# Toeplitz tables laid out once in DRAM, one load per readout table, and six of eight state copies on VectorE

## The chip, the core and the metric

The kernel runs on one core of a Trainium2 chip. TensorE (PE in the rows) does the matmuls, VectorE (DVE) and ScalarE (ACT) the elementwise work, GpSimd (POOL) a little of it, and SyncE (SP) issues every DMA of this kernel, in program order on one queue. The metric is the time of the whole kernel on the device in microseconds, lower is better. Three runs of the kernel before took 742.02, 746.75 and 749.24 us, a median of 746.75.

## What is computed

One layer of a backbone over 1024 positions of width 1024, in float32. Each large matmul is done on operands split in a high and a low half, three matmuls for one (hi times hi, hi times lo, lo times hi). Cut to what matters here:

```python
h = layer_norm(x) * (1 + scale) + shift
ua, za, ub, vb, zb, ga, gb = split(h @ w_in + b_in)      # widths 512 x5, 1024 x2
# branch a: a bidirectional state space over positions, 32 groups of 16 channels, 64 complex states
y  = s5_bidir(ua)                                        # y = D*u + C s (forward) + C s (backward)
ya = (g := gelu(y)) * sigmoid(g @ glu_w + glu_b) * silu(za)
# branch b: a gating unit in chunks of 128 positions
v  = layer_norm(gelu(vb)) * ln_g + ln_b
yb = gelu(ub) * (w_s @ v + b_s) * silu(zb)
m  = sigmoid(ga) * (ya @ w_a) + sigmoid(gb) * (yb @ w_b)
out = layer_norm(alpha * x + gate * (m @ w_out + b_out)) * ln_g2 + ln_b2
```

## The kernel before

The state space is computed in blocks of 8 positions: a scan over 160 blocks on VectorE carries the states, and within a block the output is a small Toeplitz matrix times the inputs. The projections are done in blocks of 128 output channels (`proj`: two halves of 512 positions, 24 matmuls each into one PSUM bank, `pp<block><half>`). The blocks are numbered: UB is 0 to 3, ZB 4 to 7, ZA 8 to 11, GA 12 to 19, GB 20 to 27. In the order of the program:

- The adaLN and the projection of `ua`, then UB+0 and UB+1 with the inputs of the states (`v_in`, `v_out`), which fill `vst`, the state buffer.
- UB+2 and UB+3 with the tables of the readout. `out_powers(b)` writes the output powers `kca` of channel block b to a DRAM table `cad` (512 KB for each of two directions). `kernels(b, d)` makes the Toeplitz rows in PSUM (`pk`), copies them into `wk` on ScalarE (L651, L652) and VectorE (L655, L656), and stores them to the DRAM table `wd`.
- `scan(1, 50)`: 49 steps of three VectorE instructions each (L608, L611, L612).
- The `vb` projection with positions as rows: 192 matmuls (L690 to L692) into all eight PSUM banks at once (`pvb0` to `pvb7`), so that the next projection needs a bank that an eviction has freed. Then for each of the eight banks, the evacuation with a bias on VectorE (L698), gelu on ScalarE (L699) and a layer norm (`norm_rows`: statistics on VectorE, a few small ones on GpSimd, the scaling on ScalarE, L189).
- ZB+0 and ZB+1 (`pp40`, `pp41`, `pp50`, `pp51`), with a Silu on ScalarE that goes into `zt` (L568), the gating unit (`prs` and `ps` matmuls, L712 and on), and ZB+2, ZB+3.
- The eight steps of branch b's gate (`branch(i, GB, ...)`, TensorE) over the rest of the scan (VectorE).
- The readout. `y_tables(b)` loads what one channel block needs: `ca` (two loads of 512 KB from `cad`), `mt` (the Toeplitz table; eight loads of 64 KB from `wd`, each of which spreads shifted rows over 16 partitions) and `um` (the inputs; two loads of 256 KB). `y_states(b)` copies the states out of `vst` into `z`, eight copies of 64x512 per b, four on ScalarE and four on VectorE. `y_mm(b)` does 16 times [`um` times `mt`, `z` times `ca` twice] on TensorE (L801, L803), and a gelu into `gk` on ScalarE (L805). `y_trans(b)` transposes `gk` (L813). Then ZA, the half-GLU, GA, the output projection and the last layer norm.

Weights come through `weights(key, ahead)`: a load into a `RAW` buffer, a ScalarE copy that rounds to the high half `h_` (L72), and a VectorE subtraction that gives the low half `l_` (L73). `WSP` has 6 buffers for the halves, `RAW` has 3, `G` 27, `ROW` 2 and `TMP` 4. The program is written in one order; a scheduler places the instructions on each engine's queue, and an engine takes its queue strictly in order. A DMA can start no sooner than its destination buffer is free and its turn on SyncE's queue has come.

Of the kernel before, what the change touches and what calls it, by code (L numbers as in the profile page):

```python
# [8 lines left out]
F32 = mybir.dt.float32  # L9
F32R = mybir.dt.float32r  # L10
I32 = mybir.dt.int32
AF = mybir.ActivationFunctionType
# [4 lines left out]
T = 8  # L17
# [9 lines left out]
UB, ZB, ZA, GA, GB = 0, 4, 8, 12, 20  # L27
# [8 lines left out]
def mixer_kernel(ctx: ExitStack, tc: tile.TileContext, a, out):  # L36
    nc = tc.nc
    V, S, Pl, PE = nc.vector, nc.scalar, nc.gpsimd, nc.tensor
# [3 lines left out]
    dram = ctx.enter_context(tc.tile_pool(name="dram", bufs=1, space=bass.MemoryType.DRAM))  # L42

    def pool_of(tag, bufs, dshape, ddt=F32):
        def make(name, shape=dshape, dt=ddt):
            return sb.tile(list(shape), dt, name=name, tag=tag, bufs=bufs)
        return make

    G = pool_of("g", 27, (128, 1024))
    BIG = pool_of("big", 1, (128, 2 * NSLOT * 32))  # L50
    RAW = pool_of("raw", 3, (128, 1024))
    WSP = pool_of("wsp", 6, (128, 1024), F32R)
    TMP = pool_of("tmp", 4, (128, 512))
    ROW = pool_of("row", 2, (128, 1280))
# [5 lines left out]
    def BANK(name, shape=(128, 512)):  # L60
        return psum.tile(list(shape), F32, name=name, tag="b", bufs=8)

    def dma(o, i):
        nc.sync.dma_start(o, i)
# [22 lines left out]
    def emit_load():  # L87
        key, ap, shape, eng = jobs[emitted[0]]
        emitted[0] += 1
        raw = RAW("r_" + key, shape)  # L90
        dma(raw, ap)
        hi, lo = WSP("h_" + key, shape), WSP("l_" + key, shape)
        split(hi, lo, raw, eng)
        loaded[key] = (hi, lo)

    def weights(key, ahead=2):
        i = [j[0] for j in jobs].index(key)
        while emitted[0] < min(i + 1 + ahead, len(jobs)):
            emit_load()
        return loaded[key]  # L100
# [154 lines left out]
    ud = dram.tile([4, T, 128, 160], F32, name="ud")  # L255
# [71 lines left out]
    q, w, z, sn, cs, odd, eve, sg = (r_[i] for i in range(3, 11))  # L327
# [128 lines left out]
    for j in range(2):  # L456
        t = RAW(f"xc{j}")
# [36 lines left out]
    for b in range(4):  # L494
        p = BANK(f"pcu{b}")
# [69 lines left out]
    def act_into(blk, fn, dst=None, then=None, ahead=None, mid=None):  # L565
        def evac(p, sl):
            t = dst[:, sl] if dst is not None else TMP("act")
            S.activation(t, p, fn, bias=cols[:, C_BLK + blk:C_BLK + blk + 1])  # L568
            if then is not None:
                then(t, sl)  # L570
        proj(blk, evac, ahead, mid)
# [4 lines left out]
    vm = [G("vm0")]  # L576
# [41 lines left out]
    mask = C("mask", [128, 16])  # L618
    V.tensor_reduce(mask, ident.rearrange("p (j h) -> p h j", h=16), axis=AX.X, op=OP.add)
    wd = dram.tile([32, 16, 240], F32, name="wd")  # L620

    cad = dram.tile([4, 2, 128, 1024], F32, name="cad")
    kca = {}

    def out_powers(b):
        for d in range(2):
            ca = G(f"kca{b}{d}", (128, 8, 8, 16))
            outer(ca, ROW("katmp", (128, 8, 8, 16)), V, pc, xcr, xci, b, d, OP.subtract)
            dma(cad[b, d], ca.rearrange("p g i h -> p (g i h)"))
            kca[b, d] = ca  # L630
# [3 lines left out]
    def kernels(b, d):  # L634
        if d == 0:
            pks[b] = BANK(f"pk{b}", (128, 2, 256))
        pk = pks[b]
        ca = kca[b, d]
        gg = 32 * d + 8 * b
        for k in range(4):  # L640
            for par in range(2):
                lh = bbar[:, gg + 2 * k:gg + 2 * k + 2, :].rearrange("p g h -> p (g h)")
                o = pk[32 * k:32 * k + 32, par, :]
                g = 2 * k + par
                PE.matmul(o[:, 128 * d:128 * d + 112], lh, ca[:, g, d:d + 7, :].rearrange("p i h -> p (i h)"),
                          start=True, stop=True)
                PE.matmul(o[:, 128 * d + 112:128 * d + 128], lh, xcr[:, gg + g, :], start=True, stop=True)
        if d == 0:
            return
        wk = TMP(f"wk{b}", (128, 2, 240))  # L650
        S.activation(wk[:, :, 0:112], pk[:, :, 128:240], AF.Copy)  # L651
        S.activation(wk[:, :, 128:240], pk[:, :, 0:112], AF.Copy)  # L652
        dm = TMP(f"dm{b}", (128, 3, 16))
        V.tensor_scalar(dm[:, 2, :], mask, cols[:, C_D + b:C_D + b + 1], None, op0=OP.mult)
        V.tensor_tensor(dm[:, 0:2, :], pk[:, :, 112:128], dm[:, 2, :].unsqueeze(1).to_broadcast([128, 2, 16]), op=OP.add)  # L655
        V.tensor_tensor(wk[:, :, 112:128], pk[:, :, 240:256], dm[:, 0:2, :], op=OP.add)  # L656
        for g in range(8):
            dma(wd[8 * b + g], wk[16 * g:16 * g + 16, g % 2, :])

    for i in range(2, 4):  # L660
        vm.append(G(f"vm{i}"))
    out_powers(0)
    out_powers(1)
    act_into(UB + 2, AF.Gelu_apprx_tanh, dst=vm[2])
    kernels(0, 0)
    kernels(0, 1)
    out_powers(2)
    kernels(1, 0)
    kernels(1, 1)
    out_powers(3)  # L670
    act_into(UB + 3, AF.Gelu_apprx_tanh, dst=vm[3], mid=lambda: (kernels(2, 0), kernels(2, 1)))
    kernels(3, 0)
    kernels(3, 1)

    scan(1, 50)

# [7 lines left out]
    for q in range(4):  # L684
        wh, wl = weights(f"vb{q}")
# [56 lines left out]
    for i in range(2, 4):  # L742
        def then(t, sl):
            V.tensor_tensor(vm[i][:, sl], vm[i][:, sl], t, op=OP.mult)
        act_into(ZB + i, AF.Silu, then=then)


    def branch(i, g0, w, y, then):

        banks = []  # L750

        def evac(p, sl):
            t = TMP("act")
            S.activation(t, p, AF.Sigmoid, bias=cols[:, C_BLK + g0 + i:C_BLK + g0 + i + 1])  # L754
            banks.append((t, sl))
        proj(g0 + i, evac)
        wh, wl = weights(f"{w}{i // 2}")
        cs_ = slice(128 * (i % 2), 128 * (i % 2) + 128)
        for t, sl in banks:
            p = BANK(f"pb{g0 + i}")  # L760
            for k in range(4):
                mm3(p, wh[:, k, cs_], wl[:, k, cs_], y[k][0][:, sl], y[k][1][:, sl], k == 0, k == 3)
            then(t, p, sl)


    cas, mts, ums, zs, gks, gt = {}, {}, {}, {}, {}, []

    def y_tables(b):
        for d in range(2):
            ca = (G if b == 0 else WSP)(f"ca{b}{d}", (128, 8, 8, 16), F32)  # L770
            dma(ca.rearrange("p g i h -> p (g i h)"), cad[b, d])
            cas[b, d] = ca
        mts[b] = RAW(f"mt{b}", (128, 8, 128))
        for s in range(8):
            dma(mts[b][16 * s:16 * s + 16],
                wd[8 * b:8 * b + 8, :, 16 * (7 - s):16 * (7 - s) + 128].rearrange("g h w -> h g w"))
        ums[b] = [TMP(f"um{b}{h}", (128, 4, 128)) for h in range(2)]
        for h in range(2):
            dma(ums[b][h], ud[b].rearrange("t (h g) c -> (t h) g c", g=8)[:, 4 * h:4 * h + 4, 32:160])

    def y_states(b):
        for d in range(2):
            zt = G(f"z{b}{d}", (128, 8, 128))
            o = 31 if d == 0 else 33
            for cp in range(2):
                for par in range(2):
                    dst = zt[64 * cp:64 * cp + 64, par:8:2, :]
                    src = vst[64 * par:64 * par + 64, d, o:o + 128, cp, 4 * b:4 * b + 4].rearrange("p c q -> p q c")
                    if par == 0:
                        S.activation(dst, src, AF.Copy)  # L790
                    else:
                        V.tensor_copy(dst, src)
            zs[b, d] = zt

    def y_mm(b):
        gks[b] = ROW(f"gk{b}", (128, T, 128))
        for h in range(2):
            p = BANK(f"py{b}{h}", (128, 4, 128))
            for i in range(4):
                g = 4 * h + i  # L800
                PE.matmul(p[:, i, :], ums[b][h][:, i, :], mts[b][:, g, :], start=True, stop=False)  # L801
                for d in range(2):
                    PE.matmul(p[:, i, :], zs[b, d][:, g, :], cas[b, d][:, g].rearrange("p i h -> p (i h)"),  # L803
                              start=False, stop=d == 1)
            S.activation(gks[b][:, :, 64 * h:64 * h + 64].rearrange("p t (g h) -> p g t h", h=16),  # L805
                         p.rearrange("p g (t h) -> p g t h", h=16), AF.Gelu_apprx_tanh)
# [15 lines left out]
    yb = []  # L822
# [7 lines left out]
    for i in range(8):  # L830
        mb = G(f"mb{i}")

        def then_b(t, p, sl):
            V.tensor_tensor(mb[:, sl], t, p, op=OP.mult)
        branch(i, GB, "w_b", yb, then_b)
        dma(md[i], mb)
        if i == 6:
            y_tables(0)
            y_states(0)

    y_tables(1)
    for b in range(4):
        y_mm(b)
        if b < 3:
# [42 lines left out]
    for i in range(8):  # L887
# [16 lines left out]
        if i == 4:  # L904
# [3 lines left out]
            for h in range(2):  # L908
                p = BANK(f"pga{h}")
# [72 lines left out]
    for t in range(4, 8):  # L982
        w = 512 if t < 7 else 256
# [67 lines left out]
```

## Time and profile before

| | |
|---|---|
| median of the runs | 746.75 us |
| the profiled execution's own time | 743.85 us |
| its span, first to last instruction | 742.1 us |
| TensorE busy | 710.3 us, 96% |
| VectorE busy | 465.1 us, 63% |
| ScalarE busy | 244.5 us, 33% |
| mean granted TensorE clock | 0.992 |

The span is what the trace covers; the execution's own time is 1.75 us longer, for what lies around it. A row of the timeline gives the start of a stretch of like instructions in us from the start of the span, its length, the engine, the line, what it writes and reads, and in square brackets how long the engine sat idle before it and what it was waiting for. Names there are the program's, without buffer numbers: `h_blk` is the high half of any block's weights, `pp` any projection's bank.

### The profile page before, as it was taken

What the parts mean: (1) busy time and instruction counts of PE and PEld (TensorE: products, weight loads), DVE (VectorE), ACT (ScalarE), POOL (GpSimd) and SP (SyncE); (2) the same over time, 40 slices, a digit from 0 to 9 for tenths busy, and PEclk for the clock granted to TensorE, in tenths of its full rate; (3) what the DMA queues carried; (4) which work ended last, traced back from release to release, by engine and by line L of the source; (5) the groups of instructions that cost most, each with busy time, mean ns of one, the idle gap of its engine ahead of it and who ended that gap; (6) DMA issues with size and microseconds to landing.
All of it is one profiled execution on the core that took longest, in us unless ns stands there. A gap on an engine that the chain in (4) does not pass through costs nothing.

```text
span 742.1 us, 10068 instructions
## 1 busy us (share of the span) xinstructions
PE 710.3 (96%) x3924; PEld 587.5 (79%) x3924; DVE 465.1 (63%) x1059; ACT 244.5 (33%) x348; POOL 38.5 (5%) x41
## 2 busy tenths in 40 slices
PE   3889999999999999999999979999999999999995
PEld 1656798887888888888888968888888878888885
DVE  4487963569789585899995535134543334592995
ACT  3357737751105423111121865135111211350000
POOL 1010133000001000000000000000000000000221
PEclk9999999999999999999999999999999999999998
DMA  7950273624411211121216674111353223151441
GB/s 301 346 211 30 57 207 114 192 86 150 134 57 30 76 45 52 57 86 57 85 61 193 189 211 150 50 57 57 133 179 114 86 87 112 58 187 40 157 144 69
DMA packets 40783, 87.27 MB, mean 118 GB/s; under 512 B 8352, under 2 KB 21280, under 8 KB 40736
## 3 DMA queue, kind: packets, MB, share of 16 engines
q1 hardware_dynamic: 40736, 86.63, 34.9%
q8 instruction: 31, 0.51, 0.3%
q14 instruction: 16, 0.13, 0.1%
HBM read 70.92 MB, written 15.70 MB: 117 GB/s over the span
## 4 chain that ended last, share of the span: by engine, by line
PE 87%; DVE 5%; ACT 3%; DMA 2%; issue 1%; SPq 0%; POOL 0%; DVEq 0%; ACTq 0%; POOLq 0%
PE pp L77 13%; PE pp L78 13%; PE pp L79 13%; PE po L947 4%; PE po L946 4%; PE po L945 4%; PE pb L78 4%; PE pb L79 4%; PE pb L77 4%; PE pvb L690 2%; PE pvb L691 2%; PE pvb L692 2%; PE pv L546 2%; PE py L803 2%; PE pu L77 1%; PE pm L206 1%
## 5 line engine op out<-in xcount | busy, mean ns | idle before, releaser
L77 PE MATMUL pp<-hh,h_blk 128*128 128x512 f32 x448 | 175.5, 392 | 0.0
L79 PE MATMUL pp<-hl,h_blk 128*128 128x512 f32 x448 | 174.6, 390 | 0.0
L78 PE MATMUL pp<-hh,l_blk 128*128 128x512 f32 x448 | 174.4, 389 | 0.0
L77 PEld LDWEIGHTS pp<-hh,h_blk 128*128 128x128 f32 x448 | 84.1, 188 | 18.4 <-issue 0.6
L79 PEld LDWEIGHTS pp<-hl,h_blk 128*128 128x128 f32 x448 | 84.1, 188 | 17.5
L78 PEld LDWEIGHTS pp<-hh,l_blk 128*128 128x128 f32 x448 | 84.1, 188 | 17.4 <-DVE m L894 0.2
L73 DVE TENSOR_TENSOR l_blk<-r_blk,h_blk 128x1024 fp32r<-128x1024 f32 x28 | 34.9, 1247 | 50.6 <-ACT h_blk L72 49.8
L72 ACT ACTIVATE h_blk<-r_blk 128x1024 fp32r<-128x1024 f32 x28 | 29.9, 1069 | 98.0 <-PE pp L78 49.6
L754 ACT ACTIVATE act<-pp,cols 128x512 f32<-128x512 f32 x32 | 21.8, 682 | 96.9 <-PE pp L79 73.2
L608 DVE TENSOR_TENSOR scm<-acat,vst 128x128 f32<-128x128 f32 x158 | 46.0, 291 | 9.8 <-ACT vst L548 5.0
L612 DVE TENSOR_TENSOR vst<-vst,scs 128x64 f32<-128x64 f32 x158 | 35.4, 224 | 4.8
L611 DVE TENSOR_TENSOR scs<-scm 128x64 f32<-128x64 f32 x158 | 35.4, 224 | 4.6
L945 PE MATMUL po<-wobig,mh 128*128 128x512 f32 (+1 forms) x90 | 32.9, 365 | 0.0
L946 PE MATMUL po<-wobig,mh 128*128 128x512 f32 (+1 forms) x90 | 32.9, 365 | 0.0
L947 PE MATMUL po<-wobig,ml 128*128 128x512 f32 (+1 forms) x90 | 32.9, 365 | 0.0
L77 PE MATMUL pu<-hh,uw 128*128 128x512 f32 x64 | 27.4, 433 | 2.5 <-ACT uw L72 1.9
L79 PE MATMUL pu<-hl,uw 128*128 128x512 f32 x64 | 26.5, 417 | 0.9 <-DVE hl L200 0.9
L78 PE MATMUL pu<-hh,uw 128*128 128x512 f32 x64 | 26.5, 414 | 0.0
L690 PE MATMUL pvb<-h_vb,hh 128*128 128x512 f32 x64 | 25.1, 393 | 0.0
L691 PE MATMUL pvb<-l_vb,hh 128*128 128x512 f32 x64 | 24.9, 389 | 0.0
L79 PE MATMUL pb<-yas,h_w_a 128*128 128x512 f32 x64 | 24.9, 389 | 0.0
L79 PE MATMUL pb<-ybl,h_w_b 128*128 128x512 f32 x64 | 24.9, 389 | 0.0
(341 smaller groups left out, 1332.0 us busy)
## 6 DMA issues: line engine op xcount, KB each, us to landing
r_blk<-in_w_blk SPq DMA_DIRECT2D x28, 512.0 KB, 3.4
wm<-in_wm SPq DMA_DIRECT2D x16, 512.0 KB, 7.3
x<-in_x SPq DMA_DIRECT2D x8, 512.0 KB, 6.7
cad<-kca SPq DMA_DIRECT2D x8, 512.0 KB, 2.9
md<-mb SPq DMA_DIRECT2D x8, 512.0 KB, 2.7
ca<-cad SPq DMA_DIRECT2D x8, 512.0 KB, 5.8
mb<-md SPq DMA_DIRECT2D x8, 512.0 KB, 4.5
wgt<-in_w_gate SPq DMA_DIRECT2D x8, 512.0 KB, 3.3
```

Source lines behind the costliest of these rows:

```text
L73: return first, (eng or V).tensor_tensor(lo, src, hi.bitcast(F32), op=OP.subtract)
L77: PE.matmul(o, wh, rh, start=first, stop=False)
L78: PE.matmul(o, wl, rh, start=False, stop=False)
L79: PE.matmul(o, wh, rl, start=False, stop=last)
L608: V.tensor_tensor(scm, acat.rearrange("p d (o c) q -> p d o (c q)", o=2), both(n - 1, prev).unsqueeze(2).to_broadcast([128, 2, 2, 32]), op ...
L611: V.tensor_tensor(scs4, m4[:, :, 0, :], m4[:, :, 1, :], op=OP.add)
L612: V.tensor_tensor(both(n, 160 if n == 31 else cur), both(n, cur), scs2, op=OP.add)
L690: PE.matmul(pvb[kk], hth[k][:, ks], wh[:, j, :], start=k == 0, stop=False)
L691: PE.matmul(pvb[kk], hth[k][:, ks], wl[:, j, :], start=False, stop=False)
L945: PE.matmul(p, mh, wh, start=k == 0, stop=False)
L946: PE.matmul(p, mh, wl, start=False, stop=False)
L947: PE.matmul(p, ml, wh, start=False, stop=k == 7)
```

## The change

The Toeplitz rows in `wd` are expanded once, right after each `kernels(b, 1)`, into a new DRAM table `mtd` in the layout that the readout wants (eight DRAM to DRAM copies of 64 KB per b, 32 in all), and each `mt` is then one load of 512 KB. `um` becomes one tile and one load, in a `ROW` buffer in place of two `TMP` buffers. All `ca` tiles take `WSP` buffers (those of b = 0 were in `G`), and `gk` moves from `ROW` to `G`. ScalarE does two of the eight state copies per b, VectorE six. `kernels` and `out_powers` are called in another order around UB+2 and UB+3 (`kernel_step`), `y_states(0)` comes one GB step earlier, `y_tables(1)` moves into the last GB step, and the weights `w_b3` are asked for without lookahead there.

```diff
+    mtd = dram.tile([4, 128, 8, 128], F32, name="mtd")
...
+        for s in range(8):
+            dma(mtd[b, 16 * s:16 * s + 16],
+                wd[8 * b:8 * b + 8, :, 16 * (7 - s):16 * (7 - s) + 128].rearrange("g h w -> h g w"))
...
+    def kernel_step(b):
+        kernels(b, 0)
+        kernels(b, 1)
+        if b < 2:
+            out_powers(b + 2)
+
     act_into(UB + 2, AF.Gelu_apprx_tanh, dst=vm[2])
-    kernels(0, 0)
-    kernels(0, 1)
-    out_powers(2)
-    kernels(1, 0)
-    kernels(1, 1)
-    out_powers(3)
-    act_into(UB + 3, AF.Gelu_apprx_tanh, dst=vm[3], mid=lambda: (kernels(2, 0), kernels(2, 1)))
-    kernels(3, 0)
-    kernels(3, 1)
+    kernel_step(0)
+    act_into(UB + 3, AF.Gelu_apprx_tanh, dst=vm[3], mid=lambda: kernel_step(1))
+    kernel_step(2)
+    kernel_step(3)
...
-        wh, wl = weights(f"{w}{i // 2}")
+        wh, wl = weights(f"{w}{i // 2}", 0 if g0 + i == GB + 7 else 2)
+        if mid is not None:
+            mid()
...
-            ca = (G if b == 0 else WSP)(f"ca{b}{d}", (128, 8, 8, 16), F32)
+            ca = WSP(f"ca{b}{d}", (128, 8, 8, 16), F32)
...
-        for s in range(8):
-            dma(mts[b][16 * s:16 * s + 16],
-                wd[8 * b:8 * b + 8, :, 16 * (7 - s):16 * (7 - s) + 128].rearrange("g h w -> h g w"))
-        ums[b] = [TMP(f"um{b}{h}", (128, 4, 128)) for h in range(2)]
-        for h in range(2):
-            dma(ums[b][h], ud[b].rearrange("t (h g) c -> (t h) g c", g=8)[:, 4 * h:4 * h + 4, 32:160])
+        dma(mts[b], mtd[b])
+        ums[b] = ROW(f"um{b}", (128, 8, 128))
+        dma(ums[b], ud[b].rearrange("t (h g) c -> (t h) g c", g=8)[:, :, 32:160])
...
-                    if par == 0:
+                    if par == 0 and cp == 0:
                         S.activation(dst, src, AF.Copy)
                     else:
                         V.tensor_copy(dst, src)
...
-        gks[b] = ROW(f"gk{b}", (128, T, 128))
+        gks[b] = G(f"gk{b}", (128, T, 128))
...
-        branch(i, GB, "w_b", yb, then_b)
+        branch(i, GB, "w_b", yb, then_b, mid=(lambda: y_tables(1)) if i == 7 else None)
         dma(md[i], mb)
+        if i == 5:
+            y_states(0)
         if i == 6:
             y_tables(0)
-            y_states(0)
-
-    y_tables(1)
+
```

The scheduler moves more than the diff. Three places follow; the numbers behind the names are buffer numbers, and lines from L661 on are a few higher in the changed kernel (L698 becomes L705, L699 becomes L706).

VectorE before, at the first evacuations of the `vb` banks: the low half of ZB+1's weights stands ahead of them, and steps of the scan stand between them.

```order
L611 TENSOR_TENSOR scs_1565<-scm_1564 128x64
L612 TENSOR_TENSOR vst_1086<-vst_1086,scs_1565 128x2x32
L73 TENSOR_TENSOR l_blk5_2259<-r_blk5_2256,h_blk5_2258 128x1024
L608 TENSOR_TENSOR scm_1564<-acat_109,vst_1086 128x128
L698 TENSOR_TENSOR vt0_2310<-pvb0_2086,row0_2082 128x512
L611 TENSOR_TENSOR scs_1565<-scm_1564 128x64
L698 TENSOR_TENSOR vt0_2310<-pvb1_2087,row0_2082 128x512
L612 TENSOR_TENSOR vst_1086<-vst_1086,scs_1565 128x2x32
```

VectorE in the changed kernel, at the same place and at the end of the last layer norm of the eight:

```order
L611 TENSOR_TENSOR scs_1565<-scm_1564 128x64
L612 TENSOR_TENSOR vst_1086<-vst_1086,scs_1565 128x2x32
L705 TENSOR_TENSOR vt0_2343<-pvb0_2119,row0_2115 128x512
L705 TENSOR_TENSOR vt0_2343<-pvb1_2120,row0_2115 128x512
L705 TENSOR_TENSOR vt2_2364<-pvb2_2121,row0_2115 128x512
L176 BN_STATS lv0s_2346<-vt0_2343 128x6
...
L182 TENSOR_SCALAR lv7m_2421<-lv7m_2421 128x1
L188 SCALAR_TENSOR_TENSOR lv7m_2421<-lv7m_2421 128x1
L73 TENSOR_TENSOR l_blk5_2292<-r_blk5_2289,h_blk5_2291 128x1024
```

The 49th and last step of `scan(1, 50)` now ends ahead of the first evacuation (before, 40 steps did), and the low half of ZB+1's weights has moved behind all eight layer norms.

ScalarE before, at the weights of ZB+0 and ZB+1:

```order
L72 ACTIVATE h_blk4_2204<-r_blk4_2202 128x1024
L72 ACTIVATE h_blk5_2258<-r_blk5_2256 128x1024
L699 ACTIVATE vt0_2310<-vt0_2310 128x512 x2
L189 ACTIVATE vt0_2310<-vt0_2310,lv0m_2315 128x512
L189 ACTIVATE vt0_2310<-vt0_2310,lv1m_2325 128x512
L699 ACTIVATE vt2_2331<-vt2_2331 128x512 x2
```

ScalarE in the changed kernel, where the high half of ZB+1's weights now stands:

```order
L189 ACTIVATE vt2_2364<-vt2_2364,lv2m_2369 128x512
L568 ACT_TABLE_LOAD
L568 ACTIVATE zt0_2427<-pp40_2434,cols_65 128x512
L189 ACTIVATE vt2_2364<-vt2_2364,lv3m_2379 128x512
L189 ACTIVATE vt4_2385<-vt4_2385,lv4m_2390 128x512
L189 ACTIVATE vt4_2385<-vt4_2385,lv5m_2400 128x512
L189 ACTIVATE vt6_2406<-vt6_2406,lv6m_2411 128x512
L706 ACT_TABLE_LOAD
L706 ACTIVATE vt6_2406<-vt6_2406 128x512
L568 ACT_TABLE_LOAD
L568 ACTIVATE zt0_2427<-pp41_2460,cols_65 128x512
L72 ACTIVATE h_blk5_2291<-r_blk5_2289 128x1024
```

It stands behind the Silu of `pp41`, and there are three loads of a function table in this stretch, where there was one.

SyncE before, ahead of and in the readout:

```order
L64 DMA ca20_3914<-cad_1576 128x1024
L64 DMA ca21_3916<-cad_1576 128x1024
L64 DMA mt2_3918<-wd_1575 16x8x128 x8
L64 DMA um20_3927<-ud_103 128x4x128
L64 DMA um21_3928<-ud_103 128x4x128
L64 DMA ca30_3970<-cad_1576 128x1024
```

SyncE in the changed kernel, from the first tables on:

```order
L64 DMA ca10_3853<-cad_1577 128x1024
L64 DMA ca11_3855<-cad_1577 128x1024
L64 DMA md_3125<-mb7_3798 128x1024
L64 DMA um2_3935<-ud_103 128x8x128
L64 DMA ca20_3929<-cad_1577 128x1024
L64 DMA ca21_3931<-cad_1577 128x1024
L64 DMA mt3_3980<-mtd_1576 128x1024
L64 DMA ca30_3976<-cad_1577 128x1024
```

The loads of `mt2` and `um2` are out from between the pairs of `ca`; `mt0` to `mt2` are issued during the GB steps.

## Rows read from the trace of the kernel before

**Rows 1.** The page, part 1: busy time, share, instructions.

```profile
PE 710.3 (96%) x3924; PEld 587.5 (79%) x3924; DVE 465.1 (63%) x1059; ACT 244.5 (33%) x348; POOL 38.5 (5%) x41
```

**Rows 2.** Stretches: length, busy PE, PEld, DVE, ACT, POOL; PEclk, DMA share, GB/s.

```profile
255.30:415.80 160.50, 160.50 (x817) 134.08 (x817) 126.45 (x389) 36.87 (x43) 0.00 (x0) 1.00 0.25 83
415.80:449.00 33.20, 27.43 (x226) 26.55 (x224) 15.77 (x21) 25.83 (x30) 0.00 (x0) 0.95 0.74 201
449.00:733.00 284.00, 284.00 (x1292) 236.22 (x1291) 144.88 (x172) 61.91 (x73) 10.46 (x7) 1.00 0.31 107
```

**Rows 3.** TensorE's waits in the readout: us in total, times, longest.

```profile
PE py L801 <- DMA um<-ud: 3.1, 1, 3.1
PE pg L813 <- ACT gk L805: 1.4, 2, 0.8
PE py L801 <- issue: 1.3, 1, 1.3
```

**Rows 4.** TensorE's timeline: the first ZB matmul, and what follows ZB+1.

```profile
233.52 0.39 PE L77 MATMUL pp<-hh,h_blk 128*128 128x512 f32 x1
...
255.37 1.09 PE L712 MATMUL prs<-wst,ones 128*64 128x128 f32 x16
```

**Rows 5.** VectorE's timeline: weights of ZB+0, two scan steps, the first evacuation.

```profile
213.95 1.22 DVE L73 TENSOR_TENSOR l_blk<-r_blk,h_blk 128x1024 fp32r<-128x1024 f32 x1
215.09 0.29 DVE L608 TENSOR_TENSOR scm<-acat,vst 128x128 f32<-128x128 f32 x1
...
215.93 0.29 DVE L608 TENSOR_TENSOR scm<-acat,vst 128x128 f32<-128x128 f32 x1
...
227.30 0.68 DVE L698 TENSOR_TENSOR vt<-pvb,row 128x512 f32<-128x512 f32 x1
```

**Rows 6.** ScalarE's groups, 220 to 262 us: busy us, mean ns, idle before.

```profile
L699 ACT ACTIVATE vt<-vt 128x512 f32<-128x512 f32 x8 | 4.6, 624 | 4.4 <-DVE vt L698 4.3
L72 ACT ACTIVATE h_blk<-r_blk 128x1024 fp32r<-128x1024 f32 x4 | 4.2, 1052 | 14.3 <-PE pvb L691 9.8 <-PE pp L78 4.5
L568 ACT ACTIVATE zt<-pp,cols 128x512 f32<-128x512 f32 x4 | 2.7, 681 | 1.5 <-PE pp L79 1.4
...
L189 ACT ACTIVATE vt<-vt,lv4m 128x512 f32<-128x512 f32 x1 | 0.8, 800 | 0.0
```

**Rows 7.** ScalarE's timeline around its one table load in this stretch.

```profile
239.74 1.66 ACT L699 ACTIVATE vt<-vt 128x512 f32<-128x512 f32 x3
241.41 1.28 ACT L568 ACT_TABLE_LOAD   x1
242.71 0.69 ACT L568 ACTIVATE zt<-pp,cols 128x512 f32<-128x512 f32 x1
```

**Rows 8.** TensorE's timeline in the readout, third of four channel blocks.

```profile
431.72 0.46 PE L801 MATMUL py<-mt,um 128*128 128x128 f32 x2 [3.08 <-DMA um<-ud]
...
436.10 0.39 PE L801 MATMUL py<-mt,um 128*128 128x128 f32 x2
...
436.77 0.39 PE L801 MATMUL py<-mt,um 128*128 128x128 f32 x2
```

**Rows 9.** TensorE behind that wait: length, busy (count), granted clock, DMA share, GB/s.

```profile
434.00:436.00 2.00, 2.00 (x11) 0.50 1.09 266
```

**Rows 10.** Tile ca: us from a load's issue to its landing.

```profile
DMA to landing us min/median/max: 3.5/5.8/7.5
```

**Rows 11.** Tile mt: the same for its loads.

```profile
DMA to landing us min/median/max: 2.1/5.1/6.9
```

**Rows 12.** The page, part 6: stores of the Toeplitz rows, KB each, us to landing.

```profile
wd<-wk SPq DMA_DIRECT2D x32, 15.0 KB, 1.5
```

**Rows 13.** Tile wd: stores of the Toeplitz rows, issue ns, first and last start.

```profile
L64 SPq DMA_DIRECT2D wd<-wk x32: 302/418/1467, 172.8 to 197.0; - x32
```

**Rows 14.** Tile z: the state copies, ns min/median/max, first and last start.

```profile
L792 DVE COPY z<-vst x16: 624/670/712, 407.3 to 430.3; 64x512 f32<-64x512 f32 x16
L790 ACT ACTIVATE z<-vst x16: 1052/1102/1187, 407.3 to 432.5; 64x512 f32<-64x512 f32 x16
```

More of the change, by code (lines that the diff above doesn't have):

```diff
@@ L745, in mixer_kernel, with branch @@
         act_into(ZB + i, AF.Silu, then=then)
-    def branch(i, g0, w, y, then):
+    def branch(i, g0, w, y, then, mid=None):
         banks = []
@@ L800, in y_mm @@
                 g = 4 * h + i
-                PE.matmul(p[:, i, :], ums[b][h][:, i, :], mts[b][:, g, :], start=True, stop=False)
+                PE.matmul(p[:, i, :], ums[b][:, g, :], mts[b][:, g, :], start=True, stop=False)
                 for d in range(2):
```

## The prediction

> **What bounds the kernel now.** I read the page first: TensorE is busy 710.3 of 742.1 us [rows 1], so the kernel is TensorE's stream, and an edit can gain only where that stream stops, or lose only where it makes it stop. The windows say where. From 255.3 to 415.8 us TensorE is busy all of 160.50 us, and from 449.0 to 733.0 all of 284.00 [rows 2]. In these stretches nothing on another engine is worth anything until it becomes late, and whatever is gained or lost ahead of them goes through to the end undiminished. Between them lies the readout, 33.20 us with 27.43 busy [rows 2]. The list of TensorE's waits names its holes: 3.1 us for an `um` load, 1.4 for gelus, 1.3 put down to issue, in all 5.8 [rows 3]. The timeline shows a second loss behind the longest: a group of six small matmuls takes 436.77 - 436.10 = 0.67 us at full pace, but the four groups from 431.72 to 436.10 take 4.38 us, 1.70 more than 4 x 0.67 [rows 8]; the granted clock there is 0.50, the lower of the two levels, 1.2 GHz [rows 9]. So the readout holds 5.8 + 1.7 = 7.5 us that could be gained, and no more: the rest is its own matmuls.
>
> The place to look at next is one that the diff doesn't touch. TensorE starts ZB+0 at 233.52 and is through ZB+1 at 255.37 [rows 4], 96 matmuls in 21.85 us, 0.228 us each, without a stop. It can, since VectorE evacuates the first `vb` bank at 227.30 [rows 5], six us before that bank is wanted. In the changed order that lead is spent.
>
> **The change part by part.**
>
> *Readout tables.* With `mt` one load and issued during the GB steps, SyncE has no round of eight small loads (5.1 us to landing, the median, up to 6.9 [rows 11]) between the pairs of `ca`. The wait for `um`, 3.1, and the slow clock behind it, 1.7, should go. What is late next is `ca`. All eight tiles now take `WSP` buffers: `ca1` waits for the last GB matmul (415.8), `ca2` for the end of the first `y_mm`, `ca3` for the end of the second. A `ca` lands 3.5 to 7.5 us after issue, median 5.8 [rows 10]. A `y_mm` is eight groups of 0.67, 5.4 us [rows 8], so `ca1` lands at 421.6 against a need at 421.2: 0.4 late. `ca2`, issued at 421.2, lands at 427.0, about when it is wanted, and `ca3` at 432.4 against some 434. I leave 1.3 of the 7.5 standing: 0.4 for `ca1`, 0.7 for one gelu that stays behind a weight split on ScalarE, 0.2 for a state copy ahead of a gelu. **Gain 6.2**, at most 7.1 (the 0.4 alone left), and 2 if every `ca` lands at its longest (rival B).
>
> *State copies.* A copy takes 670 ns on VectorE and 1102 on ScalarE [rows 14]. Per b, two fewer on ScalarE and two more on VectorE: VectorE has 6 x 0.67 = 4.0 us per b against a step of over 6 us of TensorE. Hidden; if not, it costs at most 2 x 0.67 per b. `gk` in `G`, `um` in `ROW` and the GB+7 lookahead are costed at nothing: TensorE's 160.5 us without a stop [rows 2] cover them, and what they would delay is a readout load, bounded above.
>
> *Copies into `mtd`.* The trace has no DRAM to DRAM copy. The nearest rows are the store of the rows (1.5 us to landing [rows 12]) and the load of the same 64 KB (2.1 to 6.9 [rows 11]). On SyncE the loads of the bias row and of ZB+1's weights stand behind them. The stores end at 197.0 [rows 13]; were all 32 copies still to come, in four rounds of eight at 6.9, the queue would be free at 224.6. The bias is wanted at about 234 and the weights not before 252 (below), so I cost them at nothing. The end on the other side is rival D.
>
> *VectorE's order at the `vb` banks.* The low half of ZB+0 was done at 213.95, and the next two scan steps start at 215.09 and 215.93, 0.84 apart [rows 5]. The order now sets the first evacuation behind the remaining 23 steps of `scan(1, 50)`: 215.09 + 23 x 0.84 = 234.4, in place of 227.30. It ends 0.6 later, at 235.0, and only then has `pp40` a bank. TensorE stops from 233.5 to 235.0, runs `pp40` and `pp41` (48 x 0.228 = 10.9) to 246.0, and then needs ZB+1's weights.
>
> *ScalarE's order.* `h_blk5` now stands behind the Silu of `pp41`. From 235.0 ScalarE has, ahead of the first table load, seven gelus of 0.624 and three norms of 0.80, 6.8 us [rows 6], with waits for the statistics of which the trace shows 4.4 before that group of gelus [rows 6]; I take 1.6, so 243.5, with 0 and 4.4 as ends. Then a load 1.28 [rows 7], a Silu 0.68, four norms 3.2, a load 1.28, the last gelu 0.62, a load 1.28, a Silu 0.68, and `h_blk5` 1.05 [rows 6]: 10.1 us, so 253.6. `l_blk5` follows on VectorE, 1.14 [rows 5], at 254.7. Two of ZB+1's matmuls can go at 253.6; the other 46 from 254.7 take 10.5 and end at 265.2, where the trace of before has 255.3: **9.9 lost**. TensorE has then stood still for 7.6 us. Behind the 3.1 us of the readout's wait the clock was down for 1.7 us' worth [rows 8, 9]; I add the same **1.7** here. Ends: without the waits for statistics and the slow clock 9.9 - 1.6 = 8.3, with 4.4 of waits 9.9 + 2.8 + 1.7 = 14.4. Nothing behind gives it back: TensorE has no idle from there to 415.8, and the scan that follows starts later by the same.
>
> **Sum:** 9.9 + 1.7 - 6.2 = **+5.4 us**. The profiled execution took 743.85 us itself, 1.75 more than its span, and would take 749.3. It lies 2.9 under the median of the runs, 746.75; on that scale I forecast **752.1**. By the ends, 8.3 - 7.1 = +1.2 and 14.4 - 6.2 = +8.2, so 748.0 to 755.0.
>
> **The rivals.**
>
> *A, faster.* ScalarE is through its norms and last gelu when `pp41` ends at 246.0, because VectorE, without scan steps between the evacuations, feeds it sooner. Then only Silu 0.68, `h_blk5` 1.05 and `l_blk5` 1.14 stand between, 2.9, beside the first 1.5, and the clock stays up: 4.4 - 7.1 = -2.7, 744.0. It decides at the second load's start: it would have to come before about 243, and the order's own 6.8 us of gelus and norms from 235.0, with load, Silu and four norms behind, speak against it. 7%.
>
> *B, readout gain lost.* Each `ca` lands at 7.5: `ca1` 2.1 late, `ca2` 1.1, the clock falls once more (1.7), with the 0.7 of the gelu 5.6 of the 7.5 are still there. Gain 1.9: 11.6 - 1.9 = +9.7, 756.4. For it: two pairs of 512 KB loads together were what the 7.5 came from. Against it: the queue no longer has the small loads beside them. 9%.
>
> *C, a table load costs more than its row.* If it must first let ScalarE's pipeline run empty, and the next instruction waits as long again as the load, three loads cost 3 x 1.28 = 3.8 more: +9.2, 755.9. Against it stands the one row here: the gelu before it ends at 241.40, the load runs from 241.41 to 242.69, the Silu starts at 242.71 [rows 7]. 11%.
>
> The Trainium skill, "ScalarE: Activation LUTs", section "What ACT_TABLE_LOAD costs", gives some 1.28 us for the load and some 1.38 us of drain beside it, 2.66 us for each switch. By that the three loads would add 3 x 1.38 = 4.1 and the time would be 756.2; the trace agrees with the 1.28 and shows no drain, so the sum goes by the trace.
>
> *D, the copies into `mtd` are slow.* Over (252.5 - 197.0 - 5.8) / 4 = 12.4 us a round, ZB+1's weights come late, and each further us costs 4: at 14 us +6.4 more, 758.5. Nothing in the rows is so slow. 3%.
>
> **How the numbers follow.** The forecast has 70%, A 7%, B 9%, C 11%, D 3%. The range 747 to 757 holds the forecast's case with its ends, B and C; A, D and the tails of the others are left out. About 1%, 7.5 us, is what a measurement of this kernel can tell from no change. Slower than 754.2: a seventh of the forecast's case (0.10), nearly all of B and C (0.18), D (0.03): 0.31. Faster than 739.3 has no case of its own; 0.04 from A, should its gains come in full and more. Within: 0.65.
>
> **What would show it.** In the profile of the changed kernel: the first evacuation near 234.4 and TensorE idle for some 1.5 us before ZB+0; three table loads between 243 and 252; TensorE idle some 7.6 us between ZB+0 and ZB+1, ended by ScalarE's `h_blk`, then VectorE's `l_blk`; a granted clock near 0.50 behind that; `prs` at 265 to 267 in place of 255.37. The readout should take some 27 us from the first `py` to the first ZA matmul with no wait over 1 us. I am wrong if ZB+1 starts without a stop, if the readout keeps a wait of 3 us, or if TensorE stops anywhere in the GB steps.

## The result and the profile after

The changed kernel takes 747.41 us (median of 20 runs, 746.22 to 750.70) where the kernel before takes 743.32 (20 runs, 740.88 to 749.24): ratio 1.006, 95% interval 1.0043 to 1.0076, so by the ratio 4.5 us slower (3.2 to 5.6); the two medians differ by 4.1. The profiled execution has a span of 748.3 us against 742.1. TensorE's stretches of the kernel after, cut where those of [rows 2] are cut (length, busy PE, PEld, DVE, ACT, POOL, clock, DMA share, GB/s):

```profile
233.00:266.50 33.50, 25.01 (x98) 19.16 (x96) 17.18 (x49) 19.49 (x26) 4.35 (x8) 0.90 0.15 47
266.50:427.00 160.50, 160.50 (x818) 134.10 (x818) 127.95 (x391) 35.72 (x42) 0.00 (x0) 1.00 0.23 79
427.00:455.20 28.20, 25.89 (x225) 25.04 (x224) 19.43 (x26) 17.31 (x22) 0.00 (x0) 1.00 0.82 275
455.20:740.00 284.80, 284.80 (x1298) 236.99 (x1297) 144.87 (x172) 61.81 (x73) 10.45 (x7) 1.00 0.30 102
```

The first is ZB+0 and ZB+1, which took 22 us without a stop [rows 4] and now takes 33.5 with 25 busy. The second and the fourth are still busy throughout, as in [rows 2]; the fourth is cut 0.8 us longer. The third is the readout, which has gone from 33.2 to 28.2. TensorE's waits answer to [rows 3] (us in total, times, longest):

```profile
PE pp L77 <- ACT h_blk L72: 6.6, 1, 6.6
...
PE pp L77 <- DVE vt L705: 1.8, 1, 1.8
PE py L809 <- DMA ca<-cad: 1.3, 2, 0.8
...
PE pg L819 <- ACT gk L811: 0.5, 1, 0.5
PE py L807 <- DMA um<-ud: 0.5, 1, 0.5
```

The two waits of `pp` did not exist before. The shorter one comes first in time. VectorE's timeline shows how it arises, against [rows 5]: the first evacuation stands at 234.43 in place of 227.30. The second line is the low half of blk5, ZB+1's weights, behind all the layer norms.

```profile
234.43 1.88 DVE L705 TENSOR_TENSOR vt<-pvb,row 128x512 f32<-128x512 f32 x3
...
252.99 1.22 DVE L73 TENSOR_TENSOR l_blk<-r_blk,h_blk 128x1024 fp32r<-128x1024 f32 x1 [1.02 <-ACT h_blk L72]
```

ScalarE's timeline shows how the longer one arises, against [rows 7]: three table loads, and the split of blk5 (its high half, L72) behind the Silu of `pp41`.

```profile
243.29 1.28 ACT L568 ACT_TABLE_LOAD   x1
244.59 0.69 ACT L568 ACTIVATE zt<-pp,cols 128x512 f32<-128x512 f32 x1
...
248.09 1.28 ACT L706 ACT_TABLE_LOAD   x1
249.39 0.63 ACT L706 ACTIVATE vt<-vt 128x512 f32<-128x512 f32 x1
250.03 1.28 ACT L568 ACT_TABLE_LOAD   x1
251.33 0.69 ACT L568 ACTIVATE zt<-pp,cols 128x512 f32<-128x512 f32 x1
251.91 1.05 ACT L72 ACTIVATE h_blk<-r_blk 128x1024 fp32r<-128x1024 f32 x1
```

TensorE's timeline has `pp50` begin at 253.01, behind its stop of 6.61 us. The window behind it (length, busy and count, clock, DMA share, GB/s) shows the granted clock at 0.50, the lower of the two levels:

```profile
253.01 1.22 PE L77 MATMUL pp<-hh,h_blk 128*128 128x512 f32 x2 [6.61 <-ACT h_blk L72]
```

```profile
254.00:256.00 2.00, 1.96 (x5) 0.50 0.35 63
```

What the reader should note is that the data asked for none of this. The loads of the bias row, which the first evacuation needs, and of `sgu_b` beside it were issued at 212.6 to 213.5 us and landed 4.0 us later (tile row), 17 us ahead of 234.43:

```profile
L64 SPq DMA_DIRECT2D row<-in_sgu_b x2: 512/556/601, 213.0 to 213.5; - x2
L64 SPq DMA_DIRECT2D row<-in_rows x1: 366/366/366, 212.6 to 212.6; - x1
...
DMA to landing us min/median/max: 3.9/4.0/4.0
```

The weights of ZB+1 were there as well. Their load is the first of the three of 219.42 on SyncE's timeline, and a weight load lands in 3.4 us (the median, page, part 6), so they lay ready some 29 us ahead of their split at 251.91:

```profile
180.58 0.35 SPq L64 DMA_DIRECT2D r_blk<-in_w_blk  x1
181.16 5.13 SPq L64 DMA_DIRECT2D mtd<-wd  x8
...
219.42 1.53 SPq L64 DMA_DIRECT2D r_blk<-in_w_blk  x3
```

```profile
r_blk<-in_w_blk SPq DMA_DIRECT2D x28, 512.0 KB, 3.4
```

The load of 180.58, ahead of the first copy into `mtd`, is that of ZB+0's weights, and their split stayed early. So what the scheduler set late here has its load behind copies on SyncE's queue. e1, e2 and e4 below fit this; how the scheduler reckons is in no trace.

### The profile page after: what moved, and what is told of

It reads as the page before. It is cut to its first block, busy times and chain, and to the rows that moved or that the text cites. A ratio compares the mean times of both kernels' runs of the same rounds, so it can differ in the third digit from the quotient of the medians.

```text
span 748.3 us, 10063 instructions
## 1 busy us (share of the span) xinstructions
PE 712.7 (95%) x3924; PEld 588.0 (79%) x3924; DVE 473.3 (63%) x1067; ACT 237.3 (32%) x342; POOL 38.3 (5%) x41
## 4 chain that ended last, share of the span: by engine, by line
PE 83%; DVE 10%; ACT 3%; DMA 2%; issue 2%; POOL 1%; SPq 0%; DVEq 0%; POOLq 0%
PE pp L77 13%; PE pp L78 13%; PE pp L79 13%; PE po L952 4%; PE po L951 4%; PE po L953 4%; PE pb L77 4%; PE pb L78 4%; PE pb L79 4%; PE pv L546 2%; DVE scm L608 2%; DVE scs L611 1%; PE py L809 1%; PE pu L77 1%; DVE vst L612 1%
## 5 line engine op out<-in xcount | busy, mean ns | idle before, releaser
L72 ACT ACTIVATE h_blk<-r_blk 128x1024 fp32r<-128x1024 f32 x28 | 29.8, 1068 | 83.1 <-PE pp L78 44.9
L77 PE MATMUL pu<-hh,uw 128*128 128x512 f32 x64 | 28.5, 451 | 2.5 <-ACT uw L72 1.9
L78 PE MATMUL pu<-hh,uw 128*128 128x512 f32 x64 | 26.9, 421 | 0.0
L698 PE MATMUL pvb<-l_vb,hh 128*128 128x512 f32 x64 | 25.0, 391 | 0.0
L699 PE MATMUL pvb<-h_vb,hl 128*128 128x512 f32 x64 | 24.9, 389 | 0.0
```

Source lines behind the costliest of these rows:

```text
L72: first = S.activation(hi, src, AF.Copy)
L77: PE.matmul(o, wh, rh, start=first, stop=False)
L78: PE.matmul(o, wl, rh, start=False, stop=False)
```

## The experiments

All kernels keep the same work in the same stages, so each span can be cut at the same points of TensorE's timeline. "Early" runs to the last matmul of the `ua` projection, "tables" from there to the first `vb` matmul, "ZB" from the last `vb` matmul to `prs`, "readout" from the first `py` to the first ZA matmul. The `vb` projection (45.1 us), `prs` to readout (160.4 to 160.5) and ZA to the end (293.0 to 293.3) are the same in all and left out. Times in us, ratios to the kernel before with 95% intervals. Each stretch is the difference of two starts given to a tenth, from one execution, so the last digit can be off by one.

| kernel | span | early | tables | ZB | readout | ratio |
|---|---|---|---|---|---|---|
| before | 742.1 | 94.3 | 93.9 | 22.1 | 33.2 | |
| changed | 748.3 | 96.5 | 91.4 | 33.5 | 28.2 | 1.006 (1.0043 to 1.0076) |
| e1 | 733.1 | 93.9 | 91.4 | 22.1 | 27.0 | 0.9898 (0.9872 to 0.9924) |
| e2 | 738.9 | 93.3 | 91.4 | 28.2 | 27.3 | 0.9965 (0.9948 to 0.9982) |
| e3 | 739.0 | 96.2 | 91.4 | 24.2 | 28.4 | 0.993 (0.9902 to 0.9958) |
| e4 | 754.8 | 94.0 | 93.9 | 40.5 | 27.9 | 1.0159 (1.0129 to 1.0189) |
| e5 | 734.1 | 93.0 | 93.8 | 22.1 | 26.6 | 0.9897 (0.9856 to 0.9938) |
| e6 | 736.9 | 94.0 | 93.8 | 22.1 | 28.4 | 0.9932 (0.9906 to 0.9958) |
| e7 | 742.7 | 96.6 | 91.5 | 22.0 | 34.0 | 0.9971 (0.9945 to 0.9997) |
| e8 | 735.8 | 92.8 | 91.4 | 22.1 | 30.8 | 0.9925 (0.9893 to 0.9957) |
| e9 | 735.4 | 96.7 | 91.4 | 22.1 | 26.6 | 0.9865 (0.9824 to 0.9907) |
| e10 | 731.4 | 92.5 | 91.4 | 22.1 | 26.8 | 0.9865 (0.9820 to 0.9911) |
| e11 | 741.6 | 94.2 | 91.4 | 30.4 | 26.9 | not timed |

"Early" is the same code in all and varies by 4.2 us between single executions; the last section shows where that comes from. Leave it out, and the other three columns give each ratio to within its interval: for the changed kernel -2.5 + 11.4 - 5.0 = +3.9 us, 1.005. The readout too is the same code in the changed kernel, e1 to e4, e6 and e11, and took 26.9 to 28.4 us. Single readouts that differ by less than 1.5 us therefore show nothing.

**e1: the copies later.** The kernel as changed, the 32 copies written ahead of ZB+2.

```diff
         for g in range(8):
             dma(wd[8 * b + g], wk[16 * g:16 * g + 16, g % 2, :])
-        for s in range(8):
-            dma(mtd[b, 16 * s:16 * s + 16],
...
+    for b in range(4):
+        expand(b)      # the same eight copies
     for i in range(2, 4):
         def then(t, sl):
```

> The changed kernel with the 32 copies into mtd written ahead of ZB+2 instead of behind each kernels(b, 1); everything else of the change stays. VectorE and ScalarE then stand at the vb banks as before the change (39 scan steps ahead of the first evacuation, both halves of blk5 ahead of the layer norms). Theory, the order of the queues is the whole loss at ZB: first evacuation near 227.3, no stop of TensorE from 233 to 255, prs near 255.4, readout 28.2 us as in the changed kernel, span 748.3 - 11.1 = 737.2, ratio to the kernel before 0.993. Rival, the copies themselves cost the time (their traffic, or SyncE's turns): they still run, beside ZB+2 and ZB+3, so weights come late there and the span stays at 745 to 748.

ZB took 22.1 without a stop. The span is 733.1 and not 737.2, since "early" was 2.6 us and the readout 1.2 shorter than in the changed kernel. The ratio came to 0.9898 for the expected 0.993. The 32 copies still ran, the last of them issued at 239.3 us. Their transfer costs TensorE nothing here; where they stand in the program does.

**e2: the bias early.** `row0` and its three loads moved ahead of `kernel_step(2)`, nothing else.

```diff
+    row0 = ROW("row0")
+    dma(row0[:, 0:512], row_bcast("rows", R_VB, 512))
+    for h in range(2): ...
     kernel_step(2)
     kernel_step(3)
     scan(1, 50)
-    row0 = ROW("row0")
...
```

> The changed kernel with the bias row and sgu_b loaded ahead of kernel_step(2); the copies stay in place. The scan steps are again spread between the evacuations (39 steps ahead of the first), but ScalarE's high half of blk5 still stands behind the Silu of pp41 and l_blk5 behind all eight norms. Only one table load. Theory, two separate waits: the bank wait of 1.84 goes (first evacuation near 227.3), the wait for blk5 stays, but shorter, since two table loads are gone: pp41 ends near 244.3, lv7's norm near 247, Silu 0.7, h_blk5 1.05, l_blk5 1.14, so TensorE idle some 4.5 us before pp50, slow clock behind; prs near 261 to 262, span 742.1 + 6.3 - 4.9 = 743.5, ratio 1.002. Rival, the wait for the bank is the cause and the rest follows from it: no stop before pp50, span 737.

With only these loads moved, 39 whole scan steps stand ahead of the first evacuation again, as before the change. The bank wait went, the wait for blk5 stayed:

```profile
244.46 0.73 PE L77 MATMUL pp<-hh,h_blk 128*128 128x512 f32 x2 [3.35 <-ACT h_blk L72]
245.72 0.58 PE L78 MATMUL pp<-hh,l_blk 128*128 128x512 f32 x1 [0.53 <-DVE l_blk L73]
```

ZB took 28.2, 6.1 over the 22.1 of before for the expected 6.3: that is what the second wait costs without the two extra table loads. The span came out 4.6 under the expected 743.5, mostly because the expectation left out the 2.5 gained in "tables"; so the ratio is 0.9965 and not 1.002.

**e3: the split early.** The reverse.

```diff
+        with ExitStack() as st:
+            if kk > 0:
+                st.enter_context(tc.issue_after(splits["blk5"][1].ins))
             V.tensor_tensor(v, pvb[kk], row0[:, 0:512], op=OP.add)
+        with tc.issue_after(splits["blk5"][0].ins):
             S.activation(v, v, AF.Gelu_apprx_tanh)
```

> The changed kernel with both halves of blk5 tied ahead of the layer norms: gelus of the vb banks behind h_blk5 on ScalarE, evacuations from the second on behind l_blk5 on VectorE. The 49 scan steps still stand ahead of the first evacuation, and the three table loads stay. Theory: the bank wait of 1.8 stays, the stop of 6.6 us before pp50 and the slow clock behind it go: prs near 255.4 + 1.8 = 257.2, span 748.3 - 9.3 = 739.0, ratio 0.996. Rival, the table loads or the late norms hold TensorE too (through zt's evacuations of the banks, or vt for the ps matmuls): prs comes, but ps waits for the last norm near 252 to 254 and later, and part of the 9.3 stays; span 742 to 746.

The span came out as the theory had it, 739.0 for 739.0, in part by luck: "early" was slow in this execution and in the one it was reckoned from. The ratio, 0.993, is lower than the expected 0.996. TensorE's only stop in ZB is the bank wait:

```profile
234.92 0.47 PE L77 MATMUL pp<-hh,h_blk 128*128 128x512 f32 x1 [1.84 <-DVE vt L708]
...
256.88 1.09 PE L723 MATMUL prs<-wst,ones 128*64 128x128 f32 x16
```

**e4: the old calling order with the copies in place.** `kernel_step` undone, nothing else.

```diff
-    kernel_step(0)
-    act_into(UB + 3, AF.Gelu_apprx_tanh, dst=vm[3], mid=lambda: kernel_step(1))
...
+    kernels(0, 0)
+    kernels(0, 1)
+    out_powers(2)
...
```

> The changed kernel with kernels and out_powers called in the order of before; the copies stay in place. The scheduler then sets the halves of blk4 too behind all eight norms (ScalarE: 8 gelus, 8 norms, h_blk4, h_blk5; VectorE: l_blk4 behind the last norm's rows), one table load, all 49 scan steps ahead of the first evacuation. Theory, the place in the queue decides: pp40 cannot start before the norms end near 247.5 and the split is done near 249.5, TensorE idle some 15 us behind the vb projection, prs near 272 to 274, span 742.1 + 17.8 - 4.9 = 755, ratio 1.017. Rival, the stall is bound to the copies' time and not to the queue: as the changed kernel, 748.

Now the split of blk4 stands behind the norms too:

```profile
248.22 1.22 PE L77 MATMUL pp<-hh,h_blk 128*128 128x512 f32 x2 [14.87 <-ACT h_blk L72]
```

ZB took 40.5 us for the same work, with one table load in the stretch and not three. The place in the queue sets the time; the rival, bound to the copies, falls. The "tables" column also went back to 93.9, which I had not expected, and e6 was made for it.

**e5: mtd alone.** The kernel before with the late copies and one load for each `mt`; `um`, `ca`, `gk`, the state copies and the calling order stay.

```diff
-        for s in range(8):
-            dma(mts[b][16 * s:16 * s + 16],
-                wd[8 * b:8 * b + 8, :, 16 * (7 - s):16 * (7 - s) + 128].rearrange("g h w -> h g w"))
+        dma(mts[b], mtd[b])
```

> The kernel before with one part of the change alone: the copies into mtd (ahead of ZB+2) and one 512 KB load for each mt. um in two loads, ca, gk, the state copies and the order of kernels and out_powers stay as before. Theory: the queue of eight small mt loads ahead of um is the readout's loss, so the 3.1 us wait and the 1.7 us of slow clock behind it go, the gelu waits and the 1.3 of issue stay: first py to first ZA matmul 33.2 - 4.8 = 28.4 us, span 742.1 - 4.8 = 737.3, ratio 0.9935. Rival, the buffers of um and ca set when the tables can land: the wait moves to um or ca and the stretch stays above 31 us, ratio over 0.997.

26.6, better than the theory's 28.4, and no worse than any run with the rest of the change beside it (26.9 to 28.4). The 3.1 us wait, the slow clock and the 1.3 of issue are gone, the last of them against the expectation and for a reason that no run shows; only the gelu waits are left:

```profile
426.18 1.09 PE L820 MATMUL pg<-ident,gk 128*128 128x128 f32 x8 [0.84 <-ACT gk L812]
...
440.27 1.09 PE L820 MATMUL pg<-ident,gk 128*128 128x128 f32 x8 [0.54 <-ACT gk L812]
```

**e6: e1 with the old calling order**, by the diff of e4.

> The kernel of e1 (copies ahead of ZB+2) with kernels and out_powers called in the order of before. Theory: the new calling order by itself shortens the stretch from the last ua matmul to the first vb matmul, which was 93.9 us before and 91.4 in the changed kernel and in e1 to e3 (0.9 us of wait for kca, the rest small switches between pk and pp matmuls): here 93.9 again, the rest as e1, ratio 0.9898 + 0.0033 = 0.993. Rival, the copies' place shortened it: 91.4 here too, ratio 0.990.

93.8 against e1's 91.4: the calling order by itself is worth 2.4 us.

**e7: all but mtd.** `mt` again from `wd`, no copies: the diff of e5 the other way round, in the changed kernel.

> The changed kernel without mtd: no copies, each mt again from wd in eight loads of 64 KB; all else of the change stays. The queues at the vb banks stand as before the change. Theory: ZB runs without a stop (22.1 us from the last vb matmul to prs), 91.4 us ahead of the vb projection, and the readout keeps a wait for a table behind the small loads: 30 to 33 us from the first py to the first ZA matmul; ratio 0.994 to 0.997. Rival, the new buffers and ca's earlier place alone take the readout's wait away: 27 to 28.5 us, ratio 0.990.

34.0, a little over the theory's 30 to 33, with a ratio at the upper end of the expected 0.994 to 0.997: the new buffers and places gain nothing. The wait has moved to `ca`, which stands behind the same small loads on SyncE's queue:

```profile
432.87 0.77 PE L805 MATMUL py<-mt,um 128*128 128x128 f32 x2 [4.80 <-DMA ca<-cad]
```

**e8: e1 with state copies four and four.**

```diff
-                    if par == 0 and cp == 0:
+                    if par == 0:
```

> The kernel of e1 with the state copies shared four and four between ScalarE and VectorE, as before the change. Theory: the copies are hidden on either engine, so the split is worth at most the gelu waits: first py to first ZA matmul within 1.3 us (2 x 0.67) of e1's 27.0, ratio 0.990 to 0.992. Rival, ScalarE's copies of 1.1 us hold up the gelus and with them the transposes and the buffers: 29 us or more, ratio 0.993 or more.

30.8, over the 29 that the rival asked for, so the rival holds in this arrangement, by another wait than it named: TensorE waits 4.1 us for the copies themselves, which ScalarE does behind gelus. The ratio, 0.9925, lies between the theory's and the rival's and settles nothing by itself.

```profile
420.27 0.49 PE L813 MATMUL py<-ca,z 128*128 128x128 f32 x2 [1.05 <-ACT z L800]
425.54 0.49 PE L813 MATMUL py<-ca,z 128*128 128x128 f32 x2 [0.31 <-ACT z L800]
427.71 0.49 PE L813 MATMUL py<-ca,z 128*128 128x128 f32 x2 [1.47 <-ACT z L800]
435.27 0.49 PE L813 MATMUL py<-ca,z 128*128 128x128 f32 x2 [1.28 <-ACT z L800]
```

In e5, where the copies are also four and four, no matmul waits for a `z`.

**e9 and e10: the parts that gain.** e9 is e5 with `kernel_step`; e10 is e9 with two and six state copies (the diff of e8 the other way round).

> The kernel of e5 (the kernel before, mtd copies ahead of ZB+2, one load for each mt) with kernels and out_powers called in the changed order; um, ca, gk and the state copies as before the change. Theory, the two parts add up: 91.4 us ahead of the vb projection, 26.6 from the first py to the first ZA matmul, ZB without a stop; 742.1 - 2.4 - 6.6 = 733.1 at the early clock of the run of before, ratio 0.988. Rival, the moved tables' loads need the changed um and ca as in e1: readout 28 us or more, ratio 0.990 or more.

> The kernel of e9 with two of the eight state copies on ScalarE and six on VectorE. Theory: with um, ca and gk as before, the copies on ScalarE stand ahead of gelus for 1.4 us of waits in e5, of which 0.9 goes: readout 25.7 us, ratio 0.987. Rival, the copies are hidden in this arrangement: 26.6 us, as e9; or VectorE's longer share comes late for a z and the stretch grows to 27 us or more.

The two parts add up, 91.4 and 26.6. The split of the copies shows no gain on top, 26.8 for the expected 25.7, as the rival had it: the gelu waits fall from 1.4 us to 0.5, and a wait of 0.9 for `um` takes their place. At 733.99 and 733.89 us these two have the lowest medians, 1.35% under the kernel before, with e9 the smaller change; e1's interval overlaps theirs.

**e11: no table switch.** The changed kernel with gelu in place of Silu in ZB+0 and ZB+1, so that these gates are another function.

```diff
-        act_into(ZB + i, AF.Silu, dst=zt[i])
+        act_into(ZB + i, AF.Gelu_apprx_tanh, dst=zt[i])
```

> The changed kernel with gelu in place of Silu for ZB+0 and ZB+1 (so these two gates are another function), which takes the three table loads out of the stretch; the rest of the queues stays as in the changed kernel. Theory, a load costs its row, 1.28 us, and nothing beside it: TensorE's stop before pp50 shrinks from 6.6 by 3.85 to 2.8 us, with less slow clock behind it; from the last vb matmul to prs 33.5 - 3.9 - 0 to 1.5 = 28.1 to 29.6 us. Rival, a load makes ScalarE wait as long again: the stop goes altogether, 26 us or less.

The stop before `pp50` was 4.01 us, over the theory's 2.8 and further still from the rival, which had it gone; ZB took 30.4 for the theory's 28.1 to 29.6 and the rival's 26 or less:

```profile
248.11 1.06 PE L77 MATMUL pp<-hh,h_blk 128*128 128x512 f32 x2 [4.01 <-ACT h_blk L72]
```

The 1.2 over the theory is not a load: ScalarE's queue had also moved the last norm (0.81) ahead of the split, and ScalarE sat idle for 0.21 and 0.31 waiting for statistics.

## Why the prediction held, and where it did not

**ZB.** This was the core of the forecast and it held. First evacuation: 234.4 predicted, 234.43 measured. Bank wait: 1.5, measured 1.84. Stop before `pp50`: 7.6, measured 6.61. What is left of the lost time, the wait for the low half and the slow clock, was put at 2.5 and measured 3.0. In all 11.6 predicted, 11.4 measured: the errors of the parts, +0.3, -1.0 and +0.5, partly cancelled, so the sum is closer than its parts. ScalarE reached the first load at 243.29 for 243.5 and the split at 251.91 for 252.55. Its waits for statistics ahead of that load were 0.56, 0.69, 0.20 and 0.20, in all 1.65; the 1.6 of the prediction was picked between 0 and 4.4 without a reason, so that it fits is luck. e1 shows that the order is the cause; e2 and e3 each take one of the two waits away.

**Readout.** 6.2 predicted, 5.0 measured here; the same code gained 4.8 to 6.3 in the seven traces that have it, so 6.2 lies in its spread, near the upper end. In this execution the term that was mis-sized is the tables that are late next: `ca` cost 1.3 as two waits for 0.4, and `um`, which I had not priced as one load, lands in 6.8 us (median) where its halves took 3.6, and cost 0.5. Rival B, at 1.9, did not come. That the gain comes from taking the small loads away is shown by e5 and e7.

```profile
mtd<-wd SPq DMA_DIRECT2D x32, 64.0 KB, 2.5
um<-ud SPq DMA_DIRECT2D x4, 512.0 KB, 6.8
```

**The calling order of the tables.** The sum gave it no line, and that is the term that failed: it gains 2.4 to 2.5 us (e4, e6). Before, TensorE waited 0.9 us for `kca` there and changed between `pk` and `pp` matmuls nine times in place of five; that the rest of the 2.4 lies in those changes is argued from the timeline, not shown.

**State copies.** I costed them at nothing, at most 1.3 per block on VectorE. In e8 ScalarE's two extra copies per block made the readout 3.8 us longer than in e1, and 2.4 longer than the slowest of the seven with that code, through ScalarE's queue, which I had not looked at. Between e9 and e10 they cost nothing that shows. So the answer depends on the arrangement; what in it decides is not shown.

**The sum.** +5.4 predicted, +3.9 by the stretches, +4.5 (3.2 to 5.6) timed. Two errors, 2.5 of missed gain and 1.2 of gain that did not come, partly cancelled. In absolute time the forecast was 752.1 and the median 747.41, only 0.4 above the lower end of the range. Of the 4.7 between them 3.4 is the base: 746.75 was the median of three runs of the kernel before, and twenty gave 743.32.

**The rivals.** A, faster, fell: the second load started at 248.09, not before 243. D, slow copies, fell: a copy lands in 2.5 us and TensorE stops for none. C, dearer table loads, fell: each load takes 1.28 us, the next instruction starts 0.02 later, and e11, without the three loads, leaves no room for more. The Trainium skill, "ScalarE: Activation LUTs", section "What ACT_TABLE_LOAD costs", has a drain of some 1.38 us beside the load; neither the rows above nor e11 show it, and the measurement decides.

**A count.** Before the change 39 whole scan steps and the first instruction of the 40th stood ahead of the first evacuation, not 40 steps; the sum does not use it.

## What to carry to other kernels

Where a scheduler places the instructions, a diff that only adds DMAs can reorder the compute engines: compare the order on each engine before and after, and look for a producer that has moved behind a consumer's own consumer, as the split of blk5 has moved behind the Silu of the projection ahead of it. Transfers that nobody needs soon belong late in the program, where no needed load stands behind them. And try the parts alone: here two of some six parts carried the whole gain that can be measured.

## What was not expected of the hardware

The first 94 us hold the same code in all kernels, and took 92.5 to 96.7 us in single executions. Most of that lies in the projection of `ua`: in all thirteen traces TensorE's idle time there is 3.5 us, while its busy time for the same matmuls goes from 66.4 to 69.9. Windows of TensorE (length, busy and count, clock, DMA share, GB/s), with the matmul ahead of which it stops from the timeline, show where. First the changed kernel:

```profile
56.53 1.65 PE L77 MATMUL pu<-hh,uw 128*128 128x512 f32 x3 [1.90 <-ACT uw L72]
```

```profile
55.00:60.00 5.00, 3.46 (x13) 0.62 0.11 20
60.00:65.00 5.00, 5.00 (x28) 0.70 0.23 85
```

Then e1:

```profile
56.52 0.96 PE L77 MATMUL pu<-hh,uw 128*128 128x512 f32 x3 [1.90 <-ACT uw L72]
```

```profile
55.00:60.00 5.00, 3.47 (x24) 1.00 0.05 15
60.00:65.00 5.00, 4.35 (x33) 1.00 0.24 90
```

The stop is the same, 1.90 us at the same place. Behind it the granted clock fell in the one execution, and 13 matmuls ran in the first window; it stayed up in the other, with 24. A clock of 0.62 and then 0.70 lacks 5 x 0.38 + 5 x 0.30 = 3.4 us of full pace over the two windows. What decides whether the clock falls behind such a stop is not shown. So two spans can differ by some 4 us, about what this change is worth, before they reach a changed line. Cut into stretches, they can still be compared.
